# Bounds by summed magnitudes on ScalarE, a separate exponential for the chunk decays, and new planner keys in a diffusion backbone step

## The chip, the cores and the metric

The kernel runs on one core of one Trainium2 chip. The core has a matrix engine (TensorE, PE in the profile), VectorE (DVE), ScalarE (ACT), GpSimd (POOL) and SyncE (SP), which here issues DMAs. Each engine works through its own instructions in order, and engines wait for each other by semaphores. The metric is the device time of one execution in microseconds (us), lower is better.

## The reference

One step of a backbone with two layers. Layer 0 mixes tokens by bidirectional gated linear attention (GLA), layer 1 by grouped-query softmax attention. There are 256 context tokens and 1024 latent tokens of width 1024.

```python
def gla_chunked(q, k, v, logg, s0):          # 4 heads, chunks of 64 tokens
    ...
    def step(S, inp):
        qi, ki, vi, gi = inp
        b = jnp.cumsum(gi, axis=2)
        b_last = b[:, :, -1:, :]
        qe = qi * jnp.exp(b)
        ke = ki * jnp.exp(-b)
        a = jnp.where(mask, jnp.einsum("bhtk,bhsk->bhts", qe, ke), 0.0)
        o = jnp.einsum("bhts,bhsv->bhtv", a, vi) + jnp.einsum("bhtk,bhkv->bhtv", qe, S)
        S = jnp.exp(b_last[:, :, 0, :])[..., None] * S + jnp.einsum(
            "bhsk,bhsv->bhkv", ki * jnp.exp(b_last - b), vi)
        return S, o
...
    o_f, s_f = gla_chunked(q, k, v, decay(0), s0[:, 0])
    o_b, s_b = gla_chunked(flip(q), flip(k), flip(v), flip(decay(1)), s0[:, 1])
    o = rms_norm(o_f + flip(o_b), onorm).reshape(B, T, GLA_VD).astype(h.dtype)
    y = (o * jax.nn.silu(gate)) @ w_out
```

Each layer is `x + gate * out` around an RMS norm with a shift and a scale that come from conditioning vectors (`w_ada`). All inputs and outputs are float32.

## The kernel before

**Numbers.** A float32 matrix product is made of three float16 products: each operand is split into a high part `hi` and a rest `lo`, and `mm3` (line 247) accumulates hi*hi, hi*lo and lo*hi. Before a split the operand is scaled by a power of two. That power comes from an upper bound of the operand's magnitudes, found by `pow2`: for weights one bound for the whole block (a tiny matmul, line 205, spreads the 128 row bounds to all partitions), for a row of tokens one bound per row. Up to now every such bound is a maximum of magnitudes, a TENSOR_REDUCE on VectorE.

**Tiling.** The 1280 tokens are 10 tiles of 128 rows. Weights come in blocks of 1024x256 by DMA into `wst` (two buffers), are scaled and split by ScalarE (`hi`) and VectorE (`lo`), and are then used from SBUF.

**The GLA loop** (`gla`) makes five passes of ten tiles, 50 slots. Pass h computes head h in one direction and adds the other direction of head h-1 (`combine`), so the fifth pass has only `combine` and the gates of head 3. A slot holds: `decay` (the log decays, split in two float16 parts), `decayed` (cumulative sums by matmul in the PSUM bank `cs`, then the exponentials `en`, `ep` and the columns `eb` that carry the decay at the chunks' ends), `intra` (the scores within chunks), `outer`, `local`, `combine` (the running states `S`, `W` by POOL line 830 and DVE lines 822 and 834; output matmul line 865), `value_gate` (PE fills a bank of the ring "mm" of two; ScalarE copies it out to `gx`, line 718, and `silu` makes the gate) and `gated`, which multiplies output and gate (lines 879 and 881) and stores the product to DRAM (`og_d`, line 882, on the SP queue). `gx` has three buffers, each free again when its store has landed.

**Work beside the loop.** `filler` puts other work into slots: products with the conditioning weights (`gemv`, line 425, tiles of 32 columns), the rank-16 projection of the context tiles (`rank`, line 647, also 32 columns), splitting the weights of layer 1 (`split_ahead`), and in slots 30, 32, 36 and 38 the four blocks of the GLA output weight (`fill_out`, jobs "wo0" to "wo3"; its bounds are lines 284 to 290, its splits lines 297 and 298).

**The crossing.** From slot 40 on rows of the GLA output are loaded back, bounded and split (`out_prep`, lines 1049 to 1053, jobs "eprep") and transposed by DMA into `hT_hi` and `hT_lo` (lines 1055 and 1056, SP queue). Two of the ten row tiles already get their output projection inside the loop ("eres", into the banks "A" and "kt"), the other eight in `gla_out`, which also projects the keys and the first queries of layer 1. Then comes `attention` (softmax, lines 1344 to 1383), and `att_out`.

**What sets the order.** The kernel is given to a planner that runs through the instructions by priority and a timeline of its own and fixes the order on every engine before the launch. `later(name)` adds the number of `LATER[name]` to the priority counter, so a larger number puts that piece behind more of what follows it in the program, a negative one ahead. These names are the keys: "combine", "gated", "jobs", "filler" and so on; names ending in 9 belong to the fifth pass, "x." to `gla_out`, "a.", "a0.", "a9." and "z." to the attention, "s." to the start.

Of the kernel before, what the change touches and what calls it, by code (L numbers as in the profile page):

```python
# [17 lines left out]
P = 128  # L18
# [32 lines left out]
LATER = {  # L51
    "loc": -30,
    "kt": 30,
    "A": -375,
    "intra": -5,
    "ks": 10,
    "combine": -15,
    "cs": -40,
    "vg": -10,
    "u": 35,  # L60
    "gated": -20,
    "decay": -25,
    "outer": 5,
    "Uc": -140,
    "a9.qr": 100,
    "a.s1": 30,
    "gate": -5,
    "a0.key": -70,
    "x.qr": -120,
    "z.val": 205,  # L70
    "o": -130,
    "x.q": -15,
    "a0.qr": 145,
    "x.prep": 20,
    "oa": 60,
    "jobs": -20,
    "a.q": -215,
    "x.mod": -200,
    "x.res": -225,
    "a.val": -20,  # L80
    "a9.gate": -20,
    "a9.q": -185,
# [1 line left out]
    "a.qr": -205,  # L84
    "a9.s1": -60,
    "a0.s1": 340,
    "pieces8": 55,
    "filler": -25,
    "a0.s0": 75,
    "at": -110,  # L90
    "a0.rest": -5,
    "a0.gate": 130,
    "silu": -395,
    "a9.s0": -55,
    "x.setup": -180,
    "a9.val": 0,
    "combine9": 280,
    "jobs9": 220,
    "filler9": -10,
    "x.key8": -55,  # L100
    "eres": 45,
    "emod": -70,
    "wo2": 185,
    "fold": 55,
    "a0.q": 35,
    "wo3": 180,
    "x.key": -95,
    "s.v": 580,
    "s.q1": 185,
    "s.r0": -155,  # L110
    "s.n2": -490,
    "s.r1": 300,
    "gated9": 30,
    "eprep": 400,
    "x.kset": 170,
    "s.q0": -25,
    "s.s0": 45,
    "s.m1": -170,
# [42 lines left out]
class K:  # L161
# [115 lines left out]

    def fill_out(self, w, st):
        nc = self.nc
        mx = self.t(self.small, [P, 2, 2], F32, "wmx")  # L280
        par = st.rearrange("p (q b j) n -> p q b j n", q=2, j=2)
        for q in range(2):
            for b in range(2):
                nc.vector.tensor_reduce(
                    mx[:, q, b : b + 1], par[:, q, :, b, :], AX.XY, ALU.max, apply_absolute_value=True
                )
        o2 = self.onorm.unsqueeze(1).to_broadcast([P, 2, 2])
        nc.vector.tensor_tensor(mx, mx, o2, ALU.mult)
        m = self.t(self.small, [P, 1], F32, "wm1")
        nc.vector.tensor_reduce(m, mx, AX.XY, ALU.max, apply_absolute_value=True)  # L290
        s, w[2] = self.pow2(m)
        so = self.t(self.small, [P, 2], F32, "wso", bufs=2)
        nc.vector.tensor_scalar(so, self.onorm, s, None, ALU.mult)
        for q in range(2):
            for b in range(2):
                hi, lo = (t.rearrange("p (q b j) n -> p q b j n", q=2, j=2)[:, q, :, b, :] for t in w[0:2])
                nc.scalar.activation(hi, par[:, q, :, b, :], AF.Copy, scale=so[:, b : b + 1])
                nc.vector.scalar_tensor_tensor(lo, par[:, q, :, b, :], so[:, b : b + 1], hi, ALU.mult, ALU.subtract)
# [453 lines left out]
    def decayed(self, h, i, g):  # L752
        nc = self.nc
        cs = self.bank("cs")[:, 0:260].rearrange("p (d k) -> p d k", d=2)
        with self.later("cs"):
            for d in range(2):
                for j in range(2):
                    nc.tensor.matmul(cs[:, d, :], g[j][:, d, :], self.cum[:, d, :], start=j == 0, stop=j == 1)
        en = self.t(self.ew, [P, 2, P], F32, "en")
        nc.scalar.activation(en, cs[:, :, 0:P], AF.Exp, scale=-1.0)  # L760
        ep = self.t(self.ew, [P, 2, 130], F32, "ep")
        nc.scalar.activation(ep, cs, AF.Exp)
        q, k = self.qkcol(h, 0, i), self.qkcol(h, 1, i)
        self.mark = nc.vector.tensor_tensor(en, en, k.unsqueeze(1).to_broadcast([P, 2, P]), ALU.mult).ins
        qe = self.t(self.tl, [P, 2, P], F32, "qe", bufs=NT + 1)
        nc.vector.tensor_tensor(qe, ep[:, :, 0:P], q.unsqueeze(1).to_broadcast([P, 2, P]), ALU.mult)
        eb = self.t(self.tl, [P, 2, 2], F32, "eb", bufs=NT + 2)
        nc.gpsimd.tensor_copy(eb, ep[:, :, P : P + 2])
        return {"qe": qe, "ke": en, "eb": eb}

    def intra(self, i, st):
# [274 lines left out]
    def out_prep(self, i, og, parts):  # L1046
        nc = self.nc
        mx = self.t(self.small, [P, 1], F32, "wm1")
        nc.vector.tensor_reduce(mx, og, AX.X, ALU.max, apply_absolute_value=True)
        s, inv = self.pow2(mx, cross=False)  # L1050
        hi, lo = parts
        nc.scalar.activation(hi, og, AF.Copy, scale=s)
# [902 lines left out]
```

## Time and profile before

| | |
|---|---|
| median of 3 runs | 1244.66 us |
| the runs | 1239.65, 1245.38, 1244.66 us |
| the profiled execution | 1240.44 us |
| its span, first to last instruction | 1238.7 us |
| mean granted TensorE clock | 0.997 |
| stages | start 0 to 80 us, loop to about 480, crossing to about 530, output projection to about 680, attention to about 1120, final projection to the end |

A profile is one execution recorded on the chip. A row of a timeline has the start in us, the duration in us, engine, line, operation, the tile written and the tiles read, the shape, the count, and in brackets how long the engine was idle before and what ended that. A row of a view by lines has the total and the mean (ns) of a group behind the first bar, and the idle time before it behind the second. A row of a view by waits names the waiting engine and line, then what it waited for: us in total, number of times, the longest. Ends of matmuls are modelled: a matmul's start is measured, but its listed duration is longer than the step to the next start, so short holes between matmuls don't show as idle time.

### The profile page before, as it was taken

To read this page: it belongs to the slowest core of one execution; us is meant where nothing else is said; L and a number is where in the kernel's file an instruction comes from. 1 tells how busy PE (TensorE), PEld (TensorE's weight loads), DVE (VectorE), ACT (ScalarE), POOL (GpSimd) and SP (SyncE) were. 2 spreads that over 40 slices of the span, in tenths; PEclk is the share of its full clock that TensorE was granted. 3 is DMA by queue.
4 is the path that set the end of the run, shared out by engine and by line. 5 is a ranking of instruction groups with operands and counts; after the bars stand their busy time and mean duration, and the time that the engine had idled before them with its cause. 6 is when DMAs were issued, how large, how long until landed. Compare 5 with 4: busy or idle time off the path is not lost. (4 is left out here: it accounts for less than half of the span.)

```text
span 1238.7 us, 22382 instructions
## 1 busy us (share of the span) xinstructions
PE 1190.6 (96%) x7990; PEld 779.1 (63%) x7990; DVE 941.7 (76%) x2177; ACT 684.6 (55%) x1694; POOL 323.7 (26%) x566
## 2 busy tenths in 40 slices
PE   5899999999999999799999999999999999989998
PEld 3467765655556566567776666766766667766444
DVE  4787778888788789986876877877767687796653
ACT  3574565666666657742333576666677676663100
POOL 0132122333221243310223444331332342310000
PEclk9999999999999999999999999999999999999999
DMA  9511567366555544479987896667957666889442
GB/s 381 215 48 74 196 195 237 113 198 203 175 186 171 184 136 144 124 189 308 205 192 187 186 174 137 134 132 145 191 126 156 128 118 137 193 152 240 153 136 85
DMA packets 318496, 210.14 MB, mean 170 GB/s; under 512 B 257158, under 2 KB 294702, under 8 KB 310064
## 3 DMA queue, kind: packets, MB, share of 16 engines
q1 hardware_dynamic: 311232, 191.18, 60.2%
q10 hardware_dynamic: 4688, 10.57, 2.3%
q0 software_dynamic: 2464, 6.95, 2.0%
q8 instruction: 63, 1.03, 0.4%
q14 instruction: 49, 0.40, 0.1%
HBM read 108.35 MB, written 38.96 MB: 119 GB/s over the span
## 5 line engine op out<-in xcount | busy, mean ns | idle before, releaser
L247 PEld LDWEIGHTS <-hT_hi 128*128 128x128 f16 x1920 | 187.6, 98 | 119.9 <-issue 3.8
L247 PE MATMUL mm<-whi,hT_hi 128*128 128x512 f16 (+1 forms) x576 | 200.1, 348 | 3.1 <-ACT gx L718 2.7
L247 PE MATMUL mm<-whi,hT_lo 128*128 128x512 f16 (+1 forms) x576 | 200.2, 347 | 0.0
L247 PE MATMUL mm<-wlo,hT_hi 128*128 128x512 f16 (+1 forms) x560 | 194.2, 347 | 0.7 <-DVE wlo L309 0.7
L247 PEld LDWEIGHTS <-whi 128*128 128x128 f16 x1232 | 120.2, 98 | 60.3 <-issue 0.9
L1344 PE MATMUL S<-kT,wst 128*128 128x512 f16 (+1 forms) x624 | 142.1, 338 | 6.5 <-ACT p L1352 6.5
L247 PE MATMUL mm<-hT_hi,whi 128*128 128x256 f16 (+1 forms) x480 | 141.0, 294 | 0.6 <-DVE og L1407 0.6
L247 PE MATMUL mm<-hT_lo,whi 128*128 128x256 f16 (+1 forms) x480 | 141.0, 294 | 0.0
L247 PE MATMUL mm<-hT_hi,wlo 128*128 128x256 f16 (+1 forms) x480 | 141.0, 294 | 0.0
L1382 DVE SCALAR_TENSOR_TENSOR phl<-p,srec,phl 128x1280 f16<-128x1280 f32 (+1 forms) x79 | 105.5, 1335 | 45.7 <-ACT phl L1381 28.4
L247 PEld LDWEIGHTS <-hT_lo 128*128 128x128 f16 x960 | 94.2, 98 | 61.3 <-issue 0.9
L1347 DVE TENSOR_REDUCE smx<-S 128x1 f32<-128x1280 f32 (+1 forms) x80 | 101.5, 1272 | 27.3 <-PE S L1344 27.1
L247 PE MATMUL mm<-PT,vh 128*128 128x256 f16 x672 | 114.8, 273 | 5.8 <-DMA PT<-phl 5.6
L1352 ACT ACTIVATE p<-S,snb,acol 128x1280 f32<-128x1280 f32 (+1 forms) x80 | 99.0, 1238 | 8.9 <-DVE phl L1382 3.8
L1344 PEld LDWEIGHTS <-wst 128*128 128x128 f16 x624 | 61.0, 98 | 57.0 <-issue 7.7
L247 PE MATMUL mm<-PT,vl 128*128 128x256 f16 x336 | 91.6, 273 | 0.0
L1379 POOL TENSOR_SCALAR phl<-p,srec 128x1280 f16<-128x1280 f32 (+1 forms) x40 | 53.7, 1342 | 104.6 <-DVE srec L1370 57.8
L247 PEld LDWEIGHTS <-wlo 128*128 128x128 f16 x616 | 60.2, 98 | 29.4
L247 PEld LDWEIGHTS <-vh 128*128 128x128 f16 x672 | 65.2, 98 | 16.0 <-DMA PT<-phl 4.4
L1172 POOL TENSOR_TENSOR rope<-hx,ropet 128x64 f32<-128x64 f32 x160 | 53.9, 367 | 76.2 <-ACT hx L1308 61.9
L270 DVE TENSOR_REDUCE wmx<-wst 128x1 f32<-128x512 f32 x104 | 65.2, 677 | 7.4 <-DMA wst<-in_att_w 5.2
L238 POOL TENSOR_TENSOR hrs<-hrsa,mhalf 128x2 f32<-128x2 f32 x50 | 40.1, 803 | 102.8 <-DVE hrsa L236 84.9
(383 smaller groups left out, 2681.0 us busy)
## 6 DMA issues: line engine op xcount, KB each, us to landing
wada<-in_w_ada SPq DMA_DIRECT2D x16, 1024.0 KB, 5.4
wst<-in_att_w SPq DMA_DIRECT2D x14, 1024.0 KB, 5.5
wst<-in_gla_w_in SPq DMA_DIRECT2D x12, 1024.0 KB, 5.5
og_d<-og POOLq DMA_DIRECT2D x40, 128.0 KB, 2.8
wst<-og_d SPq DMA_DIRECT2D x5, 1024.0 KB, 6.5
og_d<-gx SPq DMA_DIRECT2D x37, 128.0 KB, 2.1
xr<-x_d SPq DMA_DIRECT2D x9, 512.0 KB, 3.4
out<-xr ACTq DMA_DIRECT2D x17, 256.0 KB, 2.0
```

Of the source, the lines that this page charges most:

```text
L238: nc.gpsimd.tensor_tensor(r, a, self.mhalf[:, 0:w], ALU.pow)
L247: self.pe = self.nc.tensor.matmul(out, a, b, start=k == 0 and j == 0, stop=k == n - 1 and j == 2).ins
L270: nc.vector.tensor_reduce(mx[:, j : j + 1], st[:, 2 * j : 2 * j + 2, :], AX.XY, ALU.max, apply_absolute_value=True)
L1172: nc.gpsimd.tensor_tensor(tv[:, h, :, w, :], xv[:, h, :, 1 - w, :], sn[:, :, w, :], ALU.mult)
L1344: nc.tensor.matmul(S[:, a : a + n], x, y, start=m == 0, stop=m == 2)
L1347: last = nc.vector.tensor_reduce(mx, S, AX.X, ALU.max).ins
L1352: nc.scalar.activation(p, S, AF.Exp, scale=self.sexp, bias=nb, accum_out=den)
L1379: nc.gpsimd.tensor_scalar(hi, p, r, 2.0 ** 14, ALU.mult, ALU.mult)
L1382: nc.vector.scalar_tensor_tensor(lo, p, r2, hi, ALU.mult, ALU.subtract)
```

## The change

It has four parts.

1. `fill_out`: the four maxima on VectorE (one for each half of the four column pairs) are replaced by two ScalarE activations (Abs) over 128x1024 each, whose accumulator gives the sum of magnitudes of each row. A sum is an upper bound of the maximum. The two sums are multiplied by the norm's weights and added. The activation's own output is not wanted and goes into the `hi` tile, which the split overwrites.
2. `out_prep`: the maximum of each row becomes a sum by the same kind of activation, written into `hi` as well.
3. `decayed`: `ep` is now only 128 columns for each direction, and `eb` comes from an exponential of its own on ScalarE, straight from PSUM, in place of a copy on POOL.
4. Twenty-eight entries of `LATER` get other numbers (one of them, "fold", is not used by any piece).

```diff
 LATER = {
...
-    "A": -375,
+    "A": -150,
...
-    "ks": 10,
-    "combine": -15,
+    "ks": 20,
+    "combine": -65,
...
-    "gated": -20,
-    "decay": -25,
+    "gated": 145,
+    "decay": -60,
...
-    "Uc": -140,
+    "Uc": -280,
...
-    "x.qr": -120,
+    "x.qr": -305,
...
-    "o": -130,
+    "o": -280,
...
-    "oa": 60,
+    "oa": -185,
...
-    "x.mod": -200,
-    "x.res": -225,
+    "x.mod": -470,
+    "x.res": -230,
...
-    "pieces8": 55,
-    "filler": -25,
+    "pieces8": 70,
+    "filler": -30,
...
-    "at": -110,
+    "at": -165,
...
-    "silu": -395,
+    "silu": -435,
...
-    "x.setup": -180,
+    "x.setup": -295,
...
-    "combine9": 280,
-    "jobs9": 220,
-    "filler9": -10,
-    "x.key8": -55,
-    "eres": 45,
-    "emod": -70,
+    "combine9": 220,
+    "jobs9": 350,
+    "filler9": 10,
+    "x.key8": -45,
+    "eres": -100,
+    "emod": -10,
...
-    "wo3": 180,
-    "x.key": -95,
+    "wo3": 315,
+    "x.key": -55,
...
-    "gated9": 30,
-    "eprep": 400,
-    "x.kset": 170,
+    "gated9": -55,
+    "eprep": 325,
+    "x.kset": 105,
...
     def fill_out(self, w, st):
         nc = self.nc
-        mx = self.t(self.small, [P, 2, 2], F32, "wmx")
+        mx = self.t(self.small, [P, 2], F32, "wmx")
         par = st.rearrange("p (q b j) n -> p q b j n", q=2, j=2)
-        for q in range(2):
-            for b in range(2):
-                nc.vector.tensor_reduce(
-                    mx[:, q, b : b + 1], par[:, q, :, b, :], AX.XY, ALU.max, apply_absolute_value=True
-                )
-        o2 = self.onorm.unsqueeze(1).to_broadcast([P, 2, 2])
-        nc.vector.tensor_tensor(mx, mx, o2, ALU.mult)
+        for b in range(2):
+            junk = w[0][:, 4 * b : 4 * b + 4, :].rearrange("p (q j) n -> p q j n", q=2)
+            nc.scalar.activation(junk, par[:, :, b], AF.Abs, accum_out=mx[:, b : b + 1])
+        nc.vector.tensor_tensor(mx, mx, self.onorm, ALU.mult)
         m = self.t(self.small, [P, 1], F32, "wm1")
-        nc.vector.tensor_reduce(m, mx, AX.XY, ALU.max, apply_absolute_value=True)
+        nc.vector.tensor_reduce(m, mx, AX.X, ALU.add, apply_absolute_value=True)
...
-        ep = self.t(self.ew, [P, 2, 130], F32, "ep")
-        nc.scalar.activation(ep, cs, AF.Exp)
+        ep = self.t(self.ew, [P, 2, P], F32, "ep")
+        nc.scalar.activation(ep, cs[:, :, 0:P], AF.Exp)
...
-        nc.vector.tensor_tensor(qe, ep[:, :, 0:P], q.unsqueeze(1).to_broadcast([P, 2, P]), ALU.mult)
+        nc.vector.tensor_tensor(qe, ep, q.unsqueeze(1).to_broadcast([P, 2, P]), ALU.mult)
         eb = self.t(self.tl, [P, 2, 2], F32, "eb", bufs=NT + 2)
-        nc.gpsimd.tensor_copy(eb, ep[:, :, P : P + 2])
+        nc.scalar.activation(eb, cs[:, :, P : P + 2], AF.Exp)
...
         mx = self.t(self.small, [P, 1], F32, "wm1")
-        nc.vector.tensor_reduce(mx, og, AX.X, ALU.max, apply_absolute_value=True)
+        hi, lo = parts
+        nc.scalar.activation(hi, og, AF.Abs, accum_out=mx)
         s, inv = self.pow2(mx, cross=False)
-        hi, lo = parts
```

More of the change, by code (lines that the diff above doesn't have):

```diff
@@ L86 @@
     "a0.s1": 340,
-    "pieces8": 55,
-    "filler": -25,
+    "pieces8": 70,
+    "filler": -30,
     "a0.s0": 75,
-    "at": -110,
+    "at": -165,
     "a0.rest": -5,
     "a0.gate": 130,
-    "silu": -395,
+    "silu": -435,
     "a9.s0": -55,
-    "x.setup": -180,
+    "x.setup": -295,
     "a9.val": 0,
-    "combine9": 280,
-    "jobs9": 220,
-    "filler9": -10,
-    "x.key8": -55,
-    "eres": 45,
-    "emod": -70,
+    "combine9": 220,
[4 more added lines that the diff above has]
+    "emod": -10,
     "wo2": 185,
-    "fold": 55,
+    "fold": 70,
     "a0.q": 35,
-    "wo3": 180,
-    "x.key": -95,
+    "wo3": 315,
+    "x.key": -55,
     "s.v": 580,
```

## The prediction

> **What bounds the kernel now.** I read the page's head first, then the busy time of each engine by stage, then what TensorE (PE) waited for in the stages where it has idle time.
>
> ```profile
> span 1238.7 us, 22382 instructions
> ...
> PE 1190.6 (96%) x7990; PEld 779.1 (63%) x7990; DVE 941.7 (76%) x2177; ACT 684.6 (55%) x1694; POOL 323.7 (26%) x566
> ```
>
> ```profile
> 80.00:480.00 400.00, 399.11 (x2496) 247.62 (x2495) 329.28 (x897) 245.38 (x643) 113.74 (x209) 1.00 0.51 166
> 480.00:530.00 50.00, 43.03 (x302) 32.14 (x301) 47.40 (x145) 36.40 (x99) 16.60 (x26) 0.97 0.54 158
> 530.00:680.00 150.00, 150.00 (x1119) 109.49 (x1118) 109.73 (x239) 52.01 (x121) 32.60 (x60) 1.00 0.88 216
> 680.00:1120.00 440.00, 427.13 (x3084) 300.87 (x3082) 341.11 (x656) 298.66 (x752) 145.70 (x247) 1.00 0.75 152
> ```
>
> The second table has, after each stretch, its length and the busy time of PE, PE's weight loads, DVE (VectorE), ACT (ScalarE) and POOL, then the granted clock and the DMA share. TensorE is the bound of the whole program. In the gated-attention loop (80 to 480) it is idle for 400.00 - 399.11 = 0.89 us, in the output projection (530 to 680) for nothing. Work taken from DVE there buys nothing by itself, although DVE is 82% busy in the loop (329.28 of 400). Idle time that this change could reach lies in the crossing, 480 to 530: PE misses 50 - 43.03 = 6.97 us and DVE is 95% busy (47.40). The 12.87 us of the softmax attention (680 to 1120) wait for other things (below); the first 80 us contain none of the edited code.
>
> What did PE wait for in the crossing? The waits by engine, longest first:
>
> ```profile
> PE mm L247 <- ACT gx L718: 2.7, 1, 2.7
> PE z L865 <- POOL Sc L830: 1.2, 2, 1.0
> PE A L247 <- DMA hT_hi<-q: 1.0, 1, 1.0
> PE z L205 <- DVE wm L290: 0.7, 1, 0.7
> PE U L865 <- POOL Sc L830: 0.6, 1, 0.6
> PE o L865 <- POOL Sc L830: 0.5, 1, 0.5
> ```
>
> The longest, 2.7 us, is a gate tile that ACT should have copied out of PSUM. Follow it back through the DVE and ACT rows of the timeline:
>
> ```profile
> 493.61 1.27 DVE L284 TENSOR_REDUCE wmx<-wst 128x1 f32<-128x512 f32 x2
> ...
> 495.99 0.47 DVE L881 SCALAR_TENSOR_TENSOR gx<-og,ors,gx 128x256 f32<-128x256 f32 x1
> ```
>
> ```profile
> 495.64 0.42 ACT L361 ACTIVATE ls<-ls 128x256 f32<-128x256 f32 x1 [2.11 <-DVE ls L354]
> 498.96 0.47 ACT L718 ACTIVATE gx<-mm,inv_g 128x256 f32<-128x256 f32 x1 [2.90 <-DMA og_d<-gx]
> ...
> 517.70 1.13 ACT L1052 ACTIVATE q<-wst,p2s 128x1024 f16<-128x1024 f32 x1
> ```
>
> ACT stood idle, because the gate buffer's store to DRAM had not landed; that store needs L881; and L881 stood in DVE's queue behind the weight reductions of L284. The 0.7 us wait (L205 for L290) ends the same reduction chain. So 3.4 us of the idle time hang directly on L284. The wait also costs time that the busy column hides. After it the matmuls start half as often:
>
> ```profile
> 499.65 0.42 PE L247 MATMUL mm<-wlo,hT_hi 128*128 128x256 f16 x1
> 499.87 0.42 PE L247 MATMUL mm<-whi,hT_lo 128*128 128x256 f16 x1
> ...
> 502.43 0.29 PE L247 MATMUL mm<-whi,hT_lo 128*128 128x256 f16 x1
> ...
> 503.20 0.27 PE L247 MATMUL mm<-whi,hT_lo 128*128 128x256 f16 x1
> 503.31 0.27 PE L247 MATMUL mm<-whi,hT_hi 128*128 128x256 f16 x1
> ```
>
> From 499.65 to 502.43 there are 13 steps of 0.214 us, against 0.11 later: 13 x 0.105 = 1.4 us lost. The clock rows agree:
>
> ```profile
> 490.00:500.00 10.00, 6.63 (x48) 5.30 (x48) 8.77 (x34) 4.14 (x13) 2.96 (x5) 0.95 0.61 187
> 500.00:510.00 10.00, 8.83 (x57) 6.46 (x55) 8.90 (x20) 9.09 (x22) 1.95 (x3) 0.88 0.46 135
> ```
>
> Reachable in the crossing are therefore 6.97 + 1.4 = 8.4 us.
>
> **The change part by part.** Two reductions leave DVE, and ACT takes them as Abs with an accumulator.
>
> ```profile
> L284 DVE TENSOR_REDUCE wmx<-wst 128x1 f32<-128x512 f32 x8 | 5.2, 678 | 0.0
> L1049 DVE TENSOR_REDUCE wm<-wst 128x1 f32<-128x1024 f32 x4 | 4.9, 1214 | 2.2 <-DMA wst<-og_d 2.2
> ...
> L1049 DVE TENSOR_REDUCE wm<-split 128x1 f32<-128x1024 f32 x1 | 1.2, 1207 | 0.0
> ```
>
> ```profile
> L539 ACT ACTIVATE junk<-x x6: 1040/1056/1057, 4.2 to 45.5; 128x1024 f16<-128x1024 f32 x6
> L539 ACT ACTIVATION_READ_ACCUMULATOR junk<-x x6: 186/186/187, 5.2 to 46.5; 128x1 f32 x6
> ```
>
> These DVE rows are of 480 to 540: 8 reductions of fill_out (two of its four blocks) and 5 of out_prep (of ten row tiles) leave, 5.2 + 4.9 + 1.2 = 11.3 us. ACT gains 2 x 2 + 5 = 9 activations of 128x1024. The trace has no Abs of this shape; the Square with accumulator is the same form, 1.06 + 0.19 = 1.24 us, so ACT gains 11.2 us. The bounds of one are 1.06 (read hidden) and 1.4. The other two blocks of fill_out and five row tiles lie where PE is never idle: no gain, no cost.
>
> This is an exchange of loads. Over 480 to 530, counting all of it inside, DVE goes from 47.4 to 36.1 and ACT from 36.4 to 47.6. The larger load stays the same. What argues for a gain is the place: ACT was idle 2.11 and 2.90 us just where DVE was full, and its 490 to 500 row has only 4.14 busy. Of the 3.4 + 1.4 = 4.8 us I take back 4.0. The three waits for the running state (L865 for POOL Sc, 2.3 us) hang on DVE's queue as well, but also on the serial chain Sc, Wc, Sc: 1.0. The wait for the first transposed tile (1.0) sits behind three L1049 and gains the new Abs: 0.3. Bounds for these together: 0 and 8.4.
>
> The decay of each tile gets a third exponential on ACT, and POOL loses a copy.
>
> ```profile
> L762 ACT ACTIVATE ep<-cs 128x260 f32<-128x260 f32 x40 | 15.6, 390 | 0.0
> ...
> L768 POOL COPY eb<-ep 128x4 f32<-128x4 f32 x40 | 11.0, 274 | 55.9 <-ACT ep L762 54.9 <-PE kt L784 0.7 <-DVE p2m L210 0.2
> ```
>
> ```profile
> 17.41 0.22 ACT L351 ACTIVATE ls<-silu_c 128x16 f32<-128x16 f32 x1 [6.77 <-DVE silu_c L374]
> ```
>
> A tiny activation is 0.22 us, so ACT gains 40 x 0.22 = 8.8 us (bounds 0.15 and 0.3 each) and goes from 245 to about 254 of 400 in the loop: hidden by PE, which is full. POOL loses 11.0 us and, more, no longer stands in its queue until ep exists. Value for PE: 0, bounds -0.9 (all idle time of the loop) and +1.
>
> The order itself comes from the planner by the keys of LATER, and 28 of them change. In the loop PE is full, yet not at its peak everywhere. Where the projection of rank 16 (32 columns wide) is dealt out among 128-wide matmuls, each turn costs a doubled step:
>
> ```profile
> 108.20 0.28 PE L647 MATMUL mm<-hT_lo,wa1h 128*32 128x256 f16 x1
> 108.41 0.28 PE L247 MATMUL mm<-whi,hT_hi 128*128 128x256 f16 x1
> ...
> 111.20 0.28 PE L647 MATMUL mm<-hT_hi,wa1h 128*32 128x256 f16 x1
> ...
> 111.32 0.27 PE L647 MATMUL mm<-hT_hi,wa1h 128*32 128x256 f16 x1
> ```
>
> Sixteen steps of 0.215 from 107.77 to 111.20 make 3.43 us; the three triplets side by side (0.12 each, last rows) and eight others at 0.11 would be 1.2. So 2.2 us can be had if the new keys keep the narrow ones together, and as much lost if they split more. I take 1.2.
>
> In the crossing the keys move combine9 and gated9 earlier (POOL's Sc, DVE's Wc, the store on SP), and jobs9 and wo3 later: those issue the Abs and copies on ACT, and on SP the two transposes of each row tile. Behind a waiting Abs on ACT stand the gate copies that free PE's two banks; the 2.2 us that L1049 waited for its load move from DVE to ACT. I charge 0.8 for this, bounds 0 and 4.1 (one more gap like the present one, 2.7 + 1.4).
>
> The attention keeps its keys, and its idle time has other causes, rows of 680 to 1130:
>
> ```profile
> PE S L1344 <- ACT p L1352: 6.5, 7, 2.1
> PE mm L247 <- DMA PT<-phl: 5.6, 6, 2.6
> ```
>
> None is edited. A changed seam can shift it: 0, bounds -3 and +3.
>
> Sum: -4.0 - 1.0 - 0.3 - 1.2 + 0.8 = -5.7 us. The profiled execution took 1240.44 us, 1.7 around its span of 1238.7, so 1234.7. It was one of the quick ones: the runs shown are 1239.65, 1244.66 and 1245.38, median 4.2 above it. The mean of the three, 1243.2, is 2.8 above it; with that 1237.5, forecast **1238 us**.
>
> **A rule against a row.** The Trainium skill, page "TensorE: Matmul & The Clock Gate", section "Part 1: The HAM clock gate", says that the clock is halved after an idle window of about 3.4 us that runs freely. By it the 1.4 us are partly chance: a wait of 2.7 us need not cost them, and any other wait near that length may. As an estimate from that page the term lies between 0 and 1.7 us (half a window) instead of 1.4, and the sum between -4.3 and -6.0. The trace agrees that the clock fell, to 0.88 in the row above.
>
> **The rivals.** *ACT becomes the bound of the crossing.* For: 47.6 of 50 us after the exchange, as much as DVE had. Against: ACT is idle in 490 to 500 and can work ahead. Then idle time changes its owner, the sum is the loop's 1.2 at most: 1243 to 1245, say **1244**.
>
> *ACT's blocks starve PE (slower).* Place: the last pass, where PE fills a 256-wide bank with 24 matmuls in 24 x 0.11 = 2.6 us and two banks last 5.2. A fill's two Abs and four copies (0.71 each, rows below) are 2.5 + 2.8 = 5.3 us; a row tile's Abs and copy 1.24 + 1.13 = 2.4. If a fill stands in one piece in front of a gate copy, PE stops and the clock falls: 4.1 us a gap. There is one now. It decides from the third gap on: three make +8.2, and with four less the other gains, about **1252**.
>
> ```profile
> L297 ACT ACTIVATE whi<-wst,wso 128x512 f16<-128x512 f32 x4 | 2.5, 706 | 0.0
> ```
>
> *The keys do more than I credit.* All 8.4 of the crossing, 2.2 and 0.9 of the loop: -11.5, near **1232**. Against: the serial state chain stays.
>
> **How the numbers follow.** Forecast 0.46, ACT as bound 0.24, slower 0.16, larger gain 0.14. About 0.5%, 6.2 us, is what a measurement of this kernel can tell from no change; my forecast of -6.7 against the median lies at that edge, so 0.31 of its 0.46 counts as faster and 0.15 as same. Faster 0.31 + 0.14 = 0.45, same 0.15 + 0.24 = 0.39, slower 0.16. The range 1229 to 1251 takes in the bounds of the forecast (8.4 + 2.2 + 0.9 at the low end with the quick runs' level, ACT's extra gap at the high one) and leaves out most of the slower case.
>
> **What would show it.** Right: in the crossing PE's wait for gx L718 gone, no clock below 1.00, DVE under 80%, ACT near 90%; the narrow matmuls of L647 in one run; Abs with its read near 1.24 us. Wrong: PE waiting for ACT copies in the last pass, a lower clock in more than one 10 us stretch, idle time of more than 2 us in the loop, or attention idle time moved by more than 3 us.

## The result, and the profile after

The changed kernel takes 1247.43 us (median of 22 runs, 1243.16 to 1252.71), the kernel before 1242.80 us beside it (22 runs, 1239.59 to 1245.74). The ratio is 1.0040 with an interval of 1.0029 to 1.0050: slower by 0.4%, inside the 0.5% that the prediction counted as no change. The forecast was a gain of 6.7 us against the first median; the time went 4.6 us the other way, inside the stated range. The profiled execution after took 1249.04 us, that of before 1240.44, so the two traces differ by 8.6 us, 4 more than the medians. What the traces show is therefore read for its place first and for its size with that in mind.

The head of the page and the busy time by stage, after:

```profile
span 1247.3 us, 22408 instructions
...
PE 1195.5 (96%) x7990; PEld 780.1 (63%) x7990; DVE 922.9 (74%) x2151; ACT 706.6 (57%) x1770; POOL 315.1 (25%) x526
```

```profile
80.00:480.00 400.00, 394.96 (x2470) 244.54 (x2470) 325.73 (x885) 253.34 (x689) 103.97 (x171) 1.00 0.52 166
480.00:530.00 50.00, 48.49 (x349) 36.78 (x348) 41.04 (x138) 43.05 (x113) 17.39 (x24) 1.00 0.61 166
530.00:680.00 150.00, 145.51 (x1077) 105.38 (x1075) 99.06 (x224) 58.58 (x137) 29.66 (x52) 0.99 0.87 211
680.00:1120.00 440.00, 426.10 (x3036) 297.90 (x3035) 336.07 (x652) 295.82 (x750) 148.51 (x255) 0.99 0.75 148
```

Against the same rows of before, PE's idle time goes from 6.97 to 1.51 us in the crossing (50 - 48.49), and there the granted clock is 1.00 where it was 0.97. It goes from 0.89 to 5.04 us in the loop, from 0 to 4.49 us in the output projection, and from 12.87 to 13.90 us in the attention. The crossing did what it was to do; two stages where PE hardly stood still before now have holes.

The heads of the two pages divide the 8.6 us. PE's idle time over the whole span goes from 48.1 (1238.7 - 1190.6) to 51.8 us (1247.3 - 1195.5), 3.7 more. The other 4.9 us are busy time: the same 7990 matmuls take longer, because more of them ran at half clock. This second part is, it seems, mostly a matter of the two executions that were profiled. Their mean granted clocks are 0.997 (before) and 0.994 (after), but the median over the 22 runs of the changed kernel is 0.996, and over the runs of before in the three later sessions it is 0.995, 0.996 and 0.995. So the 3.7 us of idle time are probably most of the 4.6 us between the medians.

Fixed stretches move with the start, so marks in the program make a cleaner account: PE's first product of the loop, its first matmul into `y` in the output projection, and its first score of the attention. PE's timeline, before and then after:

```profile
94.76 0.60 PE L851 MATMUL A<-v,at 128*128 128x256 f32 x2
...
549.48 0.38 PE L247 MATMUL y<-whi,hT_hi 128*128 128x512 f16 x1
...
695.54 0.81 PE L1344 MATMUL S<-kT,wst 128*128 128x512 f16 x3
```

```profile
96.75 0.60 PE L848 MATMUL A<-v,at 128*128 128x256 f32 x2
...
548.48 0.38 PE L247 MATMUL y<-whi,hT_hi 128*128 128x512 f16 x1
...
700.00 0.59 PE L1341 MATMUL S<-kT,wst 128*128 128x512 f16 x2
```

Up to the first mark it is +2.0 us (in the traces of the further kernels below this mark lies between 93.3 and 96.7 us, and in a second trace of the changed kernel at 94.81). From there to `y` it is 451.73 against 454.72 us, -3.0. From `y` to the first score 151.52 against 146.06, +5.5. From the score to the end 547.3 against 543.2, +4.1. The sum is the 8.6 us.

**The crossing.** Of the waits that the prediction quoted for it, only the running state is left. Waits of PE in 480 to 530, after, all of them:

```profile
PE U L862 <- POOL Sc L827: 0.8, 1, 0.8
PE cs L862 <- POOL Sc L827: 0.6, 1, 0.6
```

The waits for `gx` (2.7 us), for the reduction chain (0.7) and for the first transposed tile (1.0) are gone. The two Abs of a `fill_out` stand on ACT between gate copies without holding one up (ACT's timeline, after; line 715 is the gate copy):

```profile
488.40 0.47 ACT L715 ACTIVATE gx<-mm,inv_g 128x256 f32<-128x256 f32 x1
...
490.88 1.04 ACT L284 ACTIVATE wada<-wst 128x1024 f16<-128x1024 f32 x1
491.83 0.19 ACT L284 ACTIVATION_READ_ACCUMULATOR wada<-wst 128x1 f32 x1
...
493.95 0.50 ACT L715 ACTIVATE gx<-mm,inv_g 128x256 f32<-128x256 f32 x1
```

An Abs with its read is 1.04 to 1.06 plus 0.19 us, as forecast from the Square. The decay's own exponential (line 765) is cheaper than the 0.22 us of the forecast: 40 of them take 7.3 us, 0.184 each.

**The output projection.** Here is the hole that the prediction did not have. ACT's timeline after, then DVE's: the last bracket is the time that the engine stood idle before the instruction, and what ended it.

```profile
576.87 1.06 ACT L1047 ACTIVATE oghl<-og 128x1024 f16<-128x1024 f32 x1 [8.11 <-DMA og<-og_d]
...
587.03 1.06 ACT L1047 ACTIVATE oghl<-og 128x1024 f16<-128x1024 f32 x1 [4.33 <-DMA og<-og_d]
...
588.09 0.89 ACT L1203 ACTIVATE xhl<-wst,asc 128x256 f16<-128x256 f32 x2
```

```profile
579.09 0.15 DVE L236 TENSOR_SCALAR nt_ra<-nt_s 128x1 f32<-128x1 f32 x1 [9.47 <-ACT hl L505]
...
588.61 0.89 DVE L1204 SCALAR_TENSOR_TENSOR xhl<-wst,asc,xhl 128x256 f16<-128x256 f32 x2 [3.88 <-ACT xhl L1203]
...
597.53 0.15 DVE L214 TENSOR_SCALAR p2c<-wm 128x1 f32<-128x1 f32 x1
```

Two new row bounds sit at the head of ACT's queue for 8.11 and 4.33 us, because the rows that they read have not landed. Nothing behind them can start: neither the sum of squares of line 505, for which DVE then stands idle 9.47 us, nor the split of line 1203, for which it stands 3.88 us. DVE's own queue is late after that. The first of the two bounds is ready at 578.0 (577.83 plus the 0.19 of its read), but the step that turns it into a scale (L214) comes only at 597.53, behind the delayed work; in the kernel before the scale of this row tile is made at 591.81. (The trace leaves buffer numbers out. That 597.53 belongs to the first of the two bounds is read from the order: the next L214 stands at 610.54, and both come before a third bound is there, at 611.3.) The transposes of the first row tile end the chain on SP's queue, after and then before:

```profile
602.07 1.25 SPq L1052 DMA_TRANSPOSE hT_hi<-oghl  x1
...
604.26 1.84 SPq L1053 DMA_TRANSPOSE hT_lo<-oghl  x1
```

```profile
595.10 2.52 SPq L1055 DMA_TRANSPOSE hT_hi<-oghl  x1
...
598.30 1.49 SPq L1056 DMA_TRANSPOSE hT_lo<-oghl  x1
```

They are 7.0 and 6.0 us later, and PE has run out of other work. PE's timeline after, and the busy time of the 10 us that follow:

```profile
607.12 0.39 PE L247 MATMUL y<-whi,hT_hi 128*128 128x512 f16 x1 [1.08 <-DMA hT_hi<-oghl]
...
610.07 0.39 PE L247 MATMUL y<-whi,hT_lo 128*128 128x512 f16 x1 [2.34 <-DMA hT_lo<-oghl]
...
612.70 0.63 PE L247 MATMUL y<-whi,hT_lo 128*128 128x512 f16 x1
613.13 0.63 PE L247 MATMUL y<-whi,hT_hi 128*128 128x512 f16 x1
```

```profile
610.00:620.00 10.00, 9.93 (x54) 5.69 (x55) 7.37 (x18) 7.17 (x19) 2.42 (x4) 0.83 1.07 248
```

PE stands 1.08 and 2.34 us, and then steps by 0.43 us where it had stepped by 0.22 (610.07 to 610.30): the granted clock of this row is 0.83, so (1 - 0.83) x 10 = 1.7 us are lost there on top. The two waits are 3.42 of the 4.49 us of this stage. The other 1.07 lie at 532, where the second row tile of the last pass waits for DVE (line 1027).

**The loop.** The longest of its new holes, on PE's and POOL's timelines after, and on POOL's before:

```profile
438.77 0.70 PE L862 MATMUL o<-Sc,qe 128*128 128x256 f32 x2 [2.29 <-POOL Sc L825]
```

```profile
437.83 0.88 POOL L825 TENSOR_SCALAR Sc<-s,eb 128x256 f32<-128x256 f32 x1 [12.32 <-DMA s<-in_state_gla]
```

```profile
435.72 0.47 POOL L828 TENSOR_SCALAR Sc<-s,eb 128x256 f32<-128x256 f32 x1 [2.98 <-DMA s<-in_state_gla]
```

Counted from the first mark, nothing moved here: POOL starts 341.1 us after it (437.83 - 96.75), before 341.0, because in both kernels it waits for the load of an initial state. After, PE's matmul `o` follows at once; before, `Sc` is there at 436.19 and `o` comes at 437.02, PE being still at work. What differs is how much PE has done until then. PE alone, from just ahead of the first mark up to `o`, before and after (the columns are the busy time with the number of matmuls, the clock, the DMA share and the rate):

```profile
94.70:437.01 342.31, 341.48 (x2133) 1.00 0.54 175
```

```profile
96.70:438.76 342.06, 338.25 (x2113) 1.00 0.54 175
```

In the same time about 20 matmuls fewer are done: by the tiles in the trace the `kt`, `U` and `A` ones of another tile, and nine of 512 columns. In PE's new order they stand behind the waiting `o` and not ahead of it, 3.2 us of work that used to cover the load.

**The seam to the attention.** Here a wait has another form. ACT's and PE's timeline after, then PE's before:

```profile
714.33 0.47 ACT L1284 ACTIVATE hx<-mm,inv_a 128x256 f32<-128x256 f32 x1 [5.46 <-DMA out<-hx]
```

```profile
716.49 0.27 PE L247 MATMUL mm<-hT_hi,whi 128*128 128x256 f16 x1 [1.98 <-ACT gx L1389]
```

```profile
711.16 1.78 PE L1344 MATMUL S<-kT,wst 128*128 128x512 f16 x9 [1.11 <-ACT p L1352]
...
716.87 1.78 PE L1344 MATMUL S<-kT,wst 128*128 128x512 f16 x9 [1.30 <-ACT p L1352]
```

After, a copy out of PSUM waits 5.46 us for a store that frees its buffer. It holds the gate copy of line 1389 behind it on ACT, and the clock of 710 to 720 is 0.86. Before, PE stands there as well, 2.41 us in two pieces, at a clock of 1.00. So the seam has cost no idle time in this trace, but some of the clock.

### The profile page after: what moved, and what is told of

Same layout as the page of the kernel before. It is cut to its first block, busy times and chain, and to the rows that moved or that the text cites. A ratio compares the mean times of both kernels' runs of the same rounds, so it can differ in the third digit from the quotient of the medians.

```text
span 1247.3 us, 22408 instructions
## 1 busy us (share of the span) xinstructions
PE 1195.5 (96%) x7990; PEld 780.1 (63%) x7990; DVE 922.9 (74%) x2151; ACT 706.6 (57%) x1770; POOL 315.1 (25%) x526
```

## The experiments

Twelve further kernels were run, one of them the changed kernel itself once more. All times are medians, ratios are to the kernel before in the same session, with 95% intervals. "Idle" is PE's idle time in the loop (80 to 480), the crossing (480 to 530) and the output projection (here 530 to 690). In these terms before has 0.89, 6.97 and 0, and the changed kernel 5.04, 1.51 and 4.49.

| run | what it is | us | ratio | idle loop / crossing / projection |
|---|---|---|---|---|
| e1 | all edits of operations, keys of before | 1260.48 | 1.0123 [1.0089, 1.0157] | 3.83 / 3.68 / 7.19 |
| e2 | operations of before, all new keys | 1253.00 | 1.0082 [1.0060, 1.0105] | 1.37 / 8.74 / 1.78 |
| e3 | changed, row bounds of the projection stage back on DVE | 1245.45 | 1.0021 [1.0001, 1.0040] | 4.88 / 1.89 / 0.62 |
| e4 | changed, the seven "x." keys of before | 1249.45 | 1.0058 [1.0037, 1.0079] | 3.77 / 1.93 / 5.50 |
| e5 | e3 and e4 together | 1242.59 | 0.9988 [0.9976, 1.0000] | 4.78 / 1.68 / 0.40 |
| e6 | e3 with `eb` copied on POOL again | 1243.99 | 1.0001 [0.9984, 1.0018] | 3.82 / 1.53 / 2.25 |
| e7 | e3 with `fill_out`'s bounds on DVE again | 1254.28 | 1.0084 [1.0068, 1.0100] | 2.38 / 8.54 / 1.29 |
| e8 | before, with Abs in `fill_out` and in the loop's row bounds | 1263.54 | 1.0160 [1.0135, 1.0185] | 6.25 / 7.03 / 13.05 |
| e9 | e5, initial state loaded straight into its buffer | 1254.52 | 1.0081 [1.0058, 1.0104] | 3.97 / 2.47 / 6.55 |
| e10 | e5, all row bounds on DVE | 1252.07 | 1.0071 [1.0047, 1.0096] | 5.04 / 2.23 / 7.01 |
| e11 | the changed kernel once more | 1248.18 | 1.0033 [1.0015, 1.0051] | 3.07 / 3.00 / 3.33 |
| e12 | e5 with the key "o" of before | 1261.31 | 1.0136 [1.0110, 1.0162] | 4.68 / 3.48 / 13.56 |

**Operations or keys? (e1, e2)** e1 is the changed kernel with every number of `LATER` as before; e2 is the kernel before with every new number.

```diff
# e1, against the changed kernel
-    "A": -150,
+    "A": -375,
...
-    "eprep": 325,
+    "eprep": 400,
# e2, against the kernel before
-    "A": -375,
+    "A": -150,
...
-    "eprep": 400,
+    "eprep": 325,
```

> All three edits of operations, with every LATER key of before. Theory A (the crossing gains because VectorE is relieved, the projection loses because the row bound of out_prep now stands in ScalarE's queue and waits for a DMA load): the crossing's idle time of TensorE falls from 7.0 us to under 4, an idle stretch of 3 us or more shows at 590 to 620, and the time lies within 3 us of before. Theory B (the new keys cause the loss, the operations are a gain): 1235 to 1239 us, ratio 0.994 to 0.997, no idle stretch in the projection.

> The operations of before with the new LATER keys. Theory A: no idle stretch at 590 to 620, because the row bounds are on VectorE; the crossing keeps VectorE near 95% busy and idle time of 5 us or more; time within 4 us of before. Theory B: the loss of the changed kernel is seen here in full or more, ratio 1.004 or above, with the idle stretch of the projection.

Each half alone is slower than both together: 1.0123 and 1.0082 against 1.0040. So the two parts aren't costs that add. (The trace of e1 is of its quickest execution, 1249.18 us, 11.3 below the median of the six, so it shows only part of what e1 loses.) The crossing separates them: with the new keys alone its idle time is 8.74 us at a clock of 0.90, with the edited operations alone 3.68 at 1.00. The hole at 435 in the loop is in e1 (2.6 us) and not in e2. The seam's one long wait is in e2 (3.7 us) and not in e1, which has two of 1.1 us. And e1 has one of its own, 5.7 and 1.4 us of PE for the key weights, which returns below. The hole near 605, which was expected in e1, isn't there; PE has already stood 7.1 us for the key weights when it comes to that place.

**The row bounds of the projection (e3).** Four of the ten row tiles get their bound in the projection stage; only those go back to DVE.

```diff
         hi, lo = parts
-        nc.scalar.activation(hi, og, AF.Abs, accum_out=mx)
+        if self.in_loop:
+            nc.scalar.activation(hi, og, AF.Abs, accum_out=mx)
+        else:
+            nc.vector.tensor_reduce(mx, og, AX.X, ALU.max, apply_absolute_value=True)
```

> The changed kernel with one thing undone: the row bounds of the four tiles that out_prep handles inside gla_out are maxima on VectorE again (the six of the loop stay Abs on ScalarE). TensorE's order is that of the changed kernel up to the first scores of the attention. Theory A: the idle 3.4 us and the halved clock at 605 to 612 go, the projection (530 to 680) has under 1.5 us idle, and the time falls by 4 to 6 us against the changed kernel, to 1242 to 1244 us, ratio to before 0.998 to 1.002. Theory B (keys): the idle stretch stays within 1 us of its size, time 1246 to 1248.

Busy time by stage and the same transposes, e3:

```profile
480.00:530.00 50.00, 48.11 (x346) 36.45 (x345) 40.91 (x140) 43.21 (x113) 17.84 (x24) 1.00 0.58 166
530.00:680.00 150.00, 149.38 (x1113) 108.60 (x1111) 107.36 (x239) 56.55 (x132) 35.24 (x62) 1.00 0.90 215
```

```profile
595.64 1.24 SPq L1056 DMA_TRANSPOSE hT_hi<-oghl  x1
...
598.79 1.64 SPq L1057 DMA_TRANSPOSE hT_lo<-oghl  x1
```

The transposes are back at 595.6 and 598.8, PE's idle time falls from 4.49 to 0.62 us, the clock is 1.00 again, and the crossing keeps its gain. The 0.62 that are left are the wait at 532. PE's order is that of the changed kernel (by the names of the tiles for all 7990 matmuls), so this is a clean test: the four Abs on ACT are the cause of this hole. In the profile the first score moves from 700.0 to 694.4 us, of which 2.1 lie in the start. The medians say less: the ratio goes from 1.0040 to 1.0021, and the two intervals overlap (a clearer pair, e4 and e5, follows). This profiled run (1241.61 us) is also the quickest of its kernel's twelve.

**The keys of the projection stage (e4), and both together (e5).**

```diff
-    "x.qr": -305,
+    "x.qr": -120,
...
-    "x.mod": -470,
-    "x.res": -230,
+    "x.mod": -200,
+    "x.res": -225,
...
-    "x.setup": -295,
+    "x.setup": -180,
...
-    "x.key8": -45,
+    "x.key8": -55,
...
-    "x.key": -55,
+    "x.key": -95,
...
-    "x.kset": 105,
+    "x.kset": 170,
```

> The changed kernel with the seven changed keys of the output projection (x.qr, x.mod, x.res, x.setup, x.key8, x.key, x.kset) set back to before; the loop's order stays that of the changed kernel. Theory A: the idle stretch near 605 stays at 2 us or more, because the Abs still waits for its load on ScalarE; time 1245 to 1248. Theory B: the stretch goes, time 1241 to 1244.

> As e3_proj_bound_dve, and besides the seven keys of the output projection are those of before. Theory S (the new x. keys open the idle stretch at the seam to the attention, 4.0 us at 709 in e3 and 3.8 at 716 with the new keys alone, absent with old x. keys): the stretch falls to 1.5 us or less, the projection stays without idle stretches over 1.2 us, and the time falls by 2 to 3 us against e3, to 1242 to 1244 us, ratio 0.998 to 1.001. Rival (the seam waits because TensorE comes to it earlier and ScalarE there is the bound whatever the keys): the stretch moves within 20 us but keeps 3 us or more, time 1244 to 1247.

With Abs on ACT (e4) the old keys don't help: the holes only change place, 2.9 us near 584 for transposes of another operand and 1.6 near 626 for those of a row tile. e4 and e5 differ in nothing but where the projection's row bounds are made, PE's order is the same in both, and here the medians are clear: 1.0058 on ACT against 0.9988 on DVE, 0.7%, with intervals that do not meet. With the bounds on DVE (e5) the old keys do help, from 1.0021 to 0.9988. The seam's one wait of 3.8 us in e3 becomes two of 1.1 and 1.6 us, as in the kernel before. That this is what the 0.3% are isn't shown: from the first score to the end the trace of e5 needs 548.8 us and that of e3 545.4. What does differ is the granted clock, with medians over the twelve runs of 0.997 in e5 and 0.9935 in e3. e5 is the best of all versions; its interval ends at 1.0000, so it is no measurable gain over before, and it lies 0.5% below the changed kernel, with intervals that do not meet. The keys alone gain nothing (1.0058 against 1.0040); once the bounds are back on DVE they are worth 0.3%.

**The decay (e6).** Theory: the hole at 435 comes from the exponential for `eb` on ACT.

```diff
-        nc.scalar.activation(eb, cs[:, :, P : P + 2], AF.Exp)
+        nc.gpsimd.tensor_copy(eb, ep[:, :, P : P + 2])
```

> As e3_proj_bound_dve, but the decays at the chunk ends are copied by POOL from a 130 column exponential again. Theory L (the separate exponential makes the planner put the output matmul of the new scan's first tile ahead of the landing of the initial state, 2.6 us at 435): that stretch goes, the loop's idle time falls from 4.9 us to under 3, and the time by 1.5 to 3 us against e3. Rival (the loop's idle time comes from the new loop keys): within 1 us of 4.9, time as e3.

The hole stays (2.2 us), so this theory falls. In the projection e6 has a wait of 1.45 us for the same transposed tile, without any Abs there: a split of the values (line 1280) sits on ACT behind a wait of 10.02 us for a load, DVE stands 10.19 us for it, and the transposes come at 598.8 and 601.4. So the Abs isn't the only operation by which a late load can do this. Its ratio of 1.0001 and the 1.0021 of e3 have overlapping intervals: a cost or gain of the separate exponential can't be told apart from none, which is what the prediction put it at.

**The weight bounds (e7).** Theory: the crossing's gain comes from `fill_out`'s reductions leaving DVE.

```diff
-        for b in range(2):
-            junk = w[0][:, 4 * b : 4 * b + 4, :].rearrange("p (q j) n -> p q j n", q=2)
-            nc.scalar.activation(junk, par[:, :, b], AF.Abs, accum_out=mx[:, b : b + 1])
+        for q in range(2):
+            for b in range(2):
+                nc.vector.tensor_reduce(
+                    mx[:, q, b : b + 1], par[:, q, :, b, :], AX.XY, ALU.max, apply_absolute_value=True
+                )
```

> As e3_proj_bound_dve, but the bounds of fill_out are maxima on VectorE again, so that of the Abs only the six of the loop's row tiles are left. Theory C (the crossing's gain is mostly the weight reductions that left VectorE's queue): the crossing, 480 to 530, has 4 us or more idle and a granted clock below 1, time 3 to 5 us above e3. Rival (keys or row bounds made the gain): idle 2.5 us or less there, time within 1.5 us of e3.

The waits of PE in 480 to 535, e7, and the busy time of the crossing by 10 us:

```profile
PE o L865 <- POOL Sc L830: 3.9, 1, 3.9
PE mm L247 <- ACT gx L718: 2.3, 2, 1.8
```

```profile
490.00:500.00 10.00, 9.41 (x76) 7.54 (x75) 9.63 (x32) 6.77 (x21) 3.47 (x4) 1.00 0.47 166
...
510.00:520.00 10.00, 5.36 (x12) 2.66 (x13) 8.75 (x26) 6.25 (x16) 6.89 (x8) 0.57 0.54 185
```

DVE is full again in 490 to 500 (9.63), PE waits for the state and for the gates as before the change, the clock drops to 0.57, and the ratio rises by 0.6% against e3, with intervals that do not meet. The theory holds for these keys. The hole at 435, on the other hand, is gone in e7. Counted in all the traces, PE has 2130 matmuls from the first mark to that `o` in before, e2 and e7, the three with the weight bounds on DVE, and none of them has the hole; it has 2111 in ten of the eleven with the Abs, which all have it (2.2 to 3.2 us); e9 is the other, with 2155 and no hole. So the order on PE goes with the hole one to one, and which order the planner makes goes with the operation in `fill_out`.

**The same Abs under the old keys (e8).** The kernel before, with `fill_out`'s Abs and the Abs of the six row tiles that are prepared in the loop, as in e3, and no other change.

```diff
-                nc.vector.tensor_reduce(
-                    mx[:, q, b : b + 1], par[:, q, :, b, :], AX.XY, ALU.max, apply_absolute_value=True
-                )
+            nc.scalar.activation(junk, par[:, :, b], AF.Abs, accum_out=mx[:, b : b + 1])
...
+        if self.in_loop:
+            nc.scalar.activation(hi, og, AF.Abs, accum_out=mx)
+        else:
+            nc.vector.tensor_reduce(mx, og, AX.X, ALU.max, apply_absolute_value=True)
```

> Before, with its own keys and its POOL copy, and only the weight bounds of fill_out and the six row bounds inside the loop as Abs on ScalarE. By theories C, L and S together it has the crossing's gain (idle under 3.5 us) without the losses of loop, projection and seam: 1237 to 1240 us, ratio 0.995 to 0.998. If the new keys are needed for the crossing's gain: idle 5 us or more there, ratio 0.999 or above.

1.0160, the slowest of all, where a gain was expected, and the crossing is no better (7.03 us at a clock of 0.90): PE waits 4.9 us for the running state and 2.1 for gate copies. So the Abs of `fill_out` is needed for the crossing's gain (e7), but doesn't bring it by itself. With the new keys it does, also with the copy on POOL (e6); with the old keys only e1 has it, which has the separate exponential and the Abs of the projection besides, and which of these counts isn't shown. The largest loss of e8 is elsewhere: PE stands 11.8 us in the projection for the key weights. This is e1's wait, twice as long.

**The hole at 435 (e9) and the remaining row bounds (e10), e11 and e12.** e9 drops the separate buffer of the initial state; e10 puts the last row bounds back on DVE; e11 is the changed kernel unaltered; e12 undoes one key.

```diff
# e9
-            s0 = self.t(self.ew, [P, DV], F32, "s0", bufs=1)
-            nc.sync.dma_start(s0, self.I["state_gla"][0, 0, d, h])
-            nc.gpsimd.tensor_scalar(s, s0, eb[:, d, 0:1], 1.0, ALU.mult, ALU.mult)
+            nc.sync.dma_start(s, self.I["state_gla"][0, 0, d, h])
+            nc.gpsimd.tensor_scalar(s, s, eb[:, d, 0:1], 1.0, ALU.mult, ALU.mult)
# e10
-        if self.in_loop:
-            nc.scalar.activation(hi, og, AF.Abs, accum_out=mx)
-        else:
-            nc.vector.tensor_reduce(mx, og, AX.X, ALU.max, apply_absolute_value=True)
+        nc.vector.tensor_reduce(mx, og, AX.X, ALU.max, apply_absolute_value=True)
# e12
-    "o": -280,
+    "o": -130,
```

> As e5_e3_old_x_keys, but the initial states are loaded straight into the running state's buffer and scaled there, so that their load no longer waits until the last pass's final state has left the shared buffer. Theory (the loop's 2.9 us at 434 is TensorE at the head of its queue with the new scan's first output matmul, while the state's load is held by the buffer): that stretch falls under 1 us and the time by 1.5 to 3 us against e5, to 1240 to 1241.5 us, ratio 0.996 to 0.998. Rival (the wait is only dealt to the next instruction, or the planner's new order costs elsewhere): time within 1.5 us of e5 or above.

> As e5_e3_old_x_keys, but all ten row bounds of out_prep are maxima on VectorE, so that only fill_out's bounds and the decay's exponential are on ScalarE. Theory C (the crossing's gain is the weight reductions): the crossing keeps under 3 us idle and a clock of 0.99 or more, time within 1.5 us of e5. Rival (the row bounds matter as much): idle 4 us or more between 480 and 540, time 3 us or more above e5.

> The changed kernel once more, beside e5 on one chip. If the profile's idle stretches are of the order and not of one execution, the stretch near 605 comes back within 1.5 us of its 3.7, that near 714 within 1 us of 2.1 and that near 436 within 1 us of 2.5; time 1246 to 1249 and 3 to 6 us above e5. If they are chance, they lie elsewhere or are missing.

> As e5_e3_old_x_keys, but the loop's key of the output matmul (o) is -130 again instead of -280, which puts that matmul later in TensorE's order. Theory (the matmul stands too early at the head of the queue): the stretch near 434 falls by 1 us or more, and the crossing keeps under 3 us idle; time 1 to 2 us below e5. Rival (with the old key the crossing's state chain waits again, as in the kernel before): the crossing's idle time rises by 2 us or more and the time is at or above e5.

e11 repeats the result: 1.0033 against 1.0040, with the same three holes (2.2 us at 433, 1.7 and 1.6 us for the transposed tile, and at the seam 3.7 us where the first trace has 2.0). Their places belong to the kernel and not to one execution. In e9 the hole at 435 is gone, but others come in the loop (2.4 us near 463, 1.3 near 300). In e12 the hole is there with 3.2 us, so undoing the key "o" doesn't remove it. In e10 the crossing keeps its gain (2.23 us, clock 1.00) without any Abs on the rows: they aren't needed for it.

What the traces of e9, e10 and e12 have in common is again a wait for the key weights (in e12 also 5.9 us for gate copies of ACT). PE's timeline, SP's and the busy time of the `y` matmuls in e10:

```profile
573.01 0.37 PE L247 MATMUL kv<-whi,hT_hi 128*128 128x256 f16 x1 [5.50 <-DMA whi<-w_kv]
```

```profile
566.88 0.53 SPq L1121 DMA_DIRECT2D whi<-w_kv  x1
```

```profile
540.00:573.00 33.00, 21.00 (x144) 0.96 0.82 170
```

and the last view for e5, up to its first key matmul at 577.02:

```profile
540.00:577.00 37.00, 29.93 (x204) 1.00 0.98 268
```

In e10 the planner put the first key matmul behind 144 matmuls of `y`, in e5 behind 204. The load of the key weights is issued at 566.88 and is there at 573.01, 6.1 us later, so the earlier place of the matmul only makes it wait. All fourteen traces fall into two classes. The five with 144 (e1, e8, e9, e10, e12) wait 6.6 to 13.1 us for key weights and take 1252 to 1264 us. Those with 204 or 216 don't wait more than 1 us for them and take 1242 to 1254. The two slowest of these are e2 and e7, whose crossing is worse than that of before. So an edit of one operation or of one key also throws this switch in the planner's order, and a comparison of two kernels is a test of the edit only where they are on the same side. For e1 and e8 against before, and for e9, e10 and e12 against e5, the times therefore say little of the edit.

## Why the prediction failed, point by point

**The gate copy's wait, the reduction wait and the half clock (-4.0).** Right in mechanism, and more came: with the state chain and the first transposes the forecast for the crossing was -5.3 us, and the traces give 5.46 us of idle time and 1.4 to 1.5 us of clock (0.97 of 50 us), 6.9 together. With the new keys `fill_out`'s four reductions are the cause (e7), and the row bounds aren't needed for it (e10). Under the old keys taking the reductions off DVE didn't suffice (e8), which the prediction didn't see. DVE came down to 41.0 of 50 (82%, forecast under 80%) and ACT only up to 43.1; PE did 349 matmuls in the stretch where it had done 302, so later work moved into it.

**The state chain (-1.0) and the first transposes (-0.3).** The chain's waits went from 2.3 to 1.4 us, and the 1.0 us for the first transposed tile is gone. Both were rightly signed; but a new wait of 1.07 us stands at 532, just behind the crossing.

**The keys keep the narrow matmuls together (-1.2).** Wrong, the order didn't do it. PE's timeline in the place that the prediction read, after:

```profile
110.40 0.28 PE L644 MATMUL mm<-hT_hi,wa1l 128*32 128x256 f16 x1
110.62 0.28 PE L247 MATMUL mm<-whi,hT_hi 128*128 128x256 f16 x1
```

They still alternate in steps of 0.215 us. Counted over the whole program, 19 turns between narrow and wide matmuls take a doubled step before and 17 after, about 0.2 us less and not 1.2. No edited key was shown to reach them.

**"The other two blocks of fill_out and five row tiles lie where PE is never idle: no gain, no cost."** This is the step that failed. Four of these row tiles lie in the projection, and the cost of an Abs is not its 1.24 us. It puts a wait for a DMA at the head of ACT's queue, 8.11 and 4.33 us, with work behind it that DVE and then PE need. The prediction charged exactly this kind of wait in the crossing (0.8 us) and left it out where PE looked covered. That PE is never idle says that its supply was in time so far, not by how much. Here the slack was less than the 6 to 7 us by which the transposes moved. e3 takes the Abs away and the hole goes. From `y` to the first score the changed kernel lost 5.5 us: 3.4 of idle time and 1.7 of clock. The traces of e3, e5 and e7 need 146.06 us there, as that of before, and that of e6 148.8; with the Abs it is 151.5 (after), 151.4 (e11) and 152.8 (e4).

**The loop at 0, bounds -0.9 and +1.** The size was wrong: 4.15 us more idle time (over 2 us in the loop was one of the prediction's signs of being wrong), of which 2.3 wait for an initial state. It is an effect of the order: about 20 matmuls changed sides of one that waits for a load. Undoing the exponential of `eb` (e6) or the key "o" (e12) doesn't remove it. In every kernel but e9 this order comes with the Abs of `fill_out`, and it goes away when these return to DVE (e7). Why the planner then puts those matmuls behind is not shown. The other holes of the loop (1.4 us for `glo` among them) are not explained.

**The attention at 0, bounds -3 and +3.** The loss after the first score is 4.1 us, above the bound, but little of it is a longer wait. PE from the first score to the end, before and after:

```profile
695.54:1238.70 543.16, 524.42 (x3558) 1.00 0.69 150
```

```profile
700.00:1247.30 547.30, 527.86 (x3558) 0.99 0.70 148
```

The idle time grows from 18.74 to 19.44 us, by 0.7; the same 3558 matmuls take 3.4 us more. In the 10 us rows up to 1240 the clock is below 0.9 twice, 0.86 at the seam and 0.83 from 1100 to 1110, behind a wait of 3.18 us for `PT`; before, the same wait was 2.60 us long and its row has 1.00. With the new "x." keys on (e2, e3, e6, e7, e11) the seam has one wait of 2.2 to 3.8 us for a gate copy. With the old ones (before, e1, e4, e5, e8, e9, e10, e12) it has two, each of 1.1 to 2.0 us, for `p`. In the whole attention the waits for `p` fell from 6.5 to 4.4 us, by about what the one for the gate copy costs (2.0), and those for `PT` went from 5.6 to 5.7.

**The rivals.** ACT did not become the bound of the crossing: it is busy 43.05 of 50 us and PE waits for no copy of it. Its blocks didn't starve PE in the last pass either. The slower rival had ACT hold up PE too, but with its busy blocks and in the last pass; what came is a waiting Abs in the projection. In the trace the change is thus the sum of a gain of some 7 us in the crossing, a loss of 4 in the loop, of about 6 in the projection (4.5 of idle time, 1.7 of clock) and of 4 behind it, 3.4 of which are clock and need not come in every execution; 2 more lie ahead of the first mark.

**The rule of the clock gate.** The Trainium skill ("TensorE: Matmul & The Clock Gate", section "Part 1: The HAM clock gate") has the clock halved after an idle window of about 3.4 us. Stops that were followed by half steps here were 2.34 us (with 1.08 shortly before) and 1.98 us long, with clocks of 0.83 and 0.86 in their rows; the 2.29 us at 438 were followed by a row of 1.00. The stop at that same place in e3, 2.48 us, was followed by rows of 0.88 and 0.95. The single stops are shorter than the window that the Trainium skill states, so here the measurement decides: stops of 2.0 to 2.5 us cost the clock in some places and not in others. The half steps lasted about 3.4 us in both places of the trace (611.4 to 614.8 and 717.1 to 720.5).

## What to carry to other kernels

Moving an operation to an idle engine also moves what it waits for: if it reads a fresh load, everything behind it in the new engine's queue waits too, so look first at those operations whose inputs have long landed (here the weight bounds, not the row bounds of the next stage). A stage in which the bounding engine never idles is not free of charge; look how late its last input comes, by the DMA's landing and the start of the consumer, before any edit there is put at nothing. With a planned order, compare the orders of two variants before reading their times: one changed key (e12 against e5) threw a switch and made the kernel 1.5% slower, several times the whole change. And before a difference of two traces is laid to an edit, compare their granted clocks with those of all the runs.

## What was not expected of the hardware

A stop of PE of 2.0 us was once followed by half clock (steps of 0.21 instead of 0.11 us from 0.65 us after the restart on), while one of 2.6 us, in the attention of the kernel before, was not. Where it came, as after the stops of 2.0, 2.3 and (before the change) 2.7 us, it cost 1.4 to 1.7 us on top of the stop, which the idle column does not show. And the first mark of the loop lies at 93.3 to 96.8 us in the fourteen traces, and at 96.75 and 94.81 in the two of the changed kernel itself: up to 3.5 us of scatter behind a start of 80 us that no edit touches, as much as most of the effects looked for here.
